# Three gate products of a hybrid decoder layer by seven half-size products, with pooled parts held in DRAM and modulation rows moved

## Chip, cores and metric

The kernel runs on one core of one Trainium2 chip. The metric is device time in microseconds of one execution of the whole layer; the median of three runs of the kernel before is 1093.55 us (1093.42 to 1094.87). Engine names as in the profile: PE is TensorE's matmul, PEld its weight load, DVE VectorE, ACT ScalarE, POOL GpSimd, SP the engine that issues most of the loads.

## The reference, cut to what matters

One layer on 512 tokens of width 1024, all in float32. The two steps around the change are the gated sum of three mixer branches and the modulation vectors:

```python
mod = (silu(c) @ w_ada + b_ada)              # six vectors of 1024
sh1, sc1, g1, sh2, sc2, g2 = split(mod, 6)
h = rms(x, norm1_w) * (1 + sc1) + sh1
z, xbc, dt, q, k, v, u, gates = split(h @ w_in)
...                                          # SSD, dilated attention, multi-scale pooling
y_ssd, y_attn = ssd @ w_ssd_out, attn @ w_attn_out
y_pool = (pooled @ w_pool_mix * pool_scale) @ w_pool_out
g_ssd, g_attn, g_pool = split(sigmoid(gates), 3)
x = x + g1 * ((g_ssd * y_ssd + g_attn * y_attn + g_pool * y_pool) @ w_out)
h = rms(x, norm2_w) * (1 + sc2) + sh2
x = x + g2 * (square(relu(h @ w_ff1)) @ w_ff2)
```

Each of the three gates is a product of h (1024 x 512) with 1024 columns of w_in; the kernel does it in two chunks of 512 columns.

## The kernel before, in words

**Products.** Activations lie feature by token: 8 blocks of 128 x 512 for 1024 features. Every float32 operand is kept as two parts, a rounded high part and the low difference (hh and hl for h), and every product is three matmuls (mm3, line 281): high weight by low input, high by high, low by high. gemm_feat (286) makes 512 output features: it streams the weights in four pairs of 128-row blocks (wstream, 271), and for each of 8 rows k and each of 4 output blocks j it issues three matmuls of 512 columns, 96 in all. A pair of weights is loaded into one of four buffers "raw" (SP's queue, 512 KB), cast by ScalarE to the high part and subtracted by VectorE to the low part, in three buffers each (wh, wl). These steps have a priority 300 instructions ahead of their place (AHEAD), evacuations 200 ahead (SOON).

**The order of work.** The program is written in one order, and a scheduler puts each engine's instructions into a fixed order by priority and readiness. Work that is to lie beside the products stands in a list, side. After each pair of weights wstream calls tick() (252), which takes one entry of side, and as many of a second list, background, as st["pace"] says; flush() (260) takes all that is left in side. Entries of background (ada_later, 239) are the 32 rows of the later modulation vectors (g1, sh2, sc2, g2): a row loads 128 x 1024 of w_ada by SP's queue (512 KB), multiplies by the condition and sums on VectorE, and adds the bias. They begin with the ssd projection, two per tick, and then one per tick (1104, 1106).

**Memory.** Besides fixed tiles there are 49 blocks of 128 x 512 (NBLK). Slots (117) hands out the block that was freed longest ago (`i = self.idle.pop(0)`), in the program's order; a tile's first write waits for the last reader of the tile before it in that block. Four double blocks have the tags L0, L1, N0 and N1, with one buffer each: they hold, one after another, copies of h in the order of residues, the attention output, the weights of the pooling mix (mix_weights, 977: half n in L{n} and N{n}), the modulation rows, and then the weights of the MLP's first product.

**The end of the mixers (1092 to 1110).** After the attention gates GA come the two halves of the pooling input (pool, 954, whose window sums run on VectorE), with the rest of the SSD beside them. pool_mix(gi) (987) makes two blocks of 12 matmuls in all per group of windows, and splits them by ScalarE and VectorE into ph_ and pl_: 16 blocks that stay until the pool projection. Then follow, for each of two chunks, the gate GS, flush(), and project(w_ssd_out), and for each of two chunks the gate GP and project(w_pool_out). gate (730) is gemm_feat and a Sigmoid on the way out; project (734) is gemm_feat, a product with the gate and a sum into the 8 blocks "mixed".

**Seven products.** The MLP does six of its eight chunks of w_ff1 by seven products of half-size blocks in place of eight (seven_products, 1302): with the input sums that input_sums (1283) makes once into 16 blocks tx and ty, and with sums of weight blocks in L and N, 7 x 24 = 168 matmuls of 256 columns make a chunk. A chunk needs all four of its weight tiles (two in L0 and L1, two in raw). The sums of the input are four pieces (rows k and k + 4): six steps and four splits each, and four blocks for the time being.

Of the kernel before, what the change touches and what calls it, by code (L numbers as in the profile page):

```python
# [98 lines left out]
def kernel(ctx: ExitStack, tc: tile.TileContext, a: dict, out: bass.AP, dbg=None):  # L99
# [139 lines left out]
    def ada_later(part, k):  # L239
        def go():  # L240
            o = modv[:, part - 2, k : k + 1]
            w = exp.tile([P, 2, T], F32, tag=("L0", "L1", "N0", "N1")[k % 4], name=uid("wada"))
            nc.sync.dma_start(w, a["w_ada"][part * 8 + k].rearrange("p (i t) -> p i t", i=2))
            V.scalar_tensor_tensor(w, w, 1.0, crow2, ALU.mult, ALU.mult, accum_out=o)
            V.tensor_tensor(o, o, vc("b_ada", part * 8 + k), ALU.add)
        return go


    background = [ada_later(part, k) for part in (2, 3, 4, 5) for k in range(8)]
    side, st, edges = [], {}, []  # L250

    def tick():
        fs = side[:1] + background[: st.get("pace", 0)]
        del side[:1], background[: st.get("pace", 0)]

        with tc.issue_after(edges[0].ins), tc.issue_after(edges[1].ins):
            for f in fs:
                f()
# [468 lines left out]

    mixed, mh, ml = [], [], []

    def gate(c, ch):  # L730
        ps = gemm_feat(w_in, 8, c + ch, hh, hl)
        return evac(ps, "sg", AF.Sigmoid)
# [254 lines left out]
    def pool_mix(gi):  # L987
        wh, wl = mixw[gi]
        for m in range(2):
            ps = psm("mix")  # L990
            cs = slice(m * P, (m + 1) * P)
            for k in range(2):
                mm3(ps, wh[:, k, cs], wl[:, k, cs], dh[2 * gi + k], dl[2 * gi + k], k == 0, k == 1)
            x, y = blk("poolh", F32R), blk("pooll", F32R)
            S.activation(x, ps, AF.Copy, scale=vc("pool_scale", gi * 2 + m))
            V.scalar_tensor_tensor(y, ps, vc("pool_scale", gi * 2 + m), x.bitcast(F32), ALU.mult, ALU.subtract)
            free(ps)
            ph_.append(x)
            pl_.append(y)
# [4 lines left out]
    def pieces(gen):  # L1004

        def step():
            next(gen, None)
        return step

    def do(gen, n):  # L1010
        side.extend([pieces(gen)] * n)
# [48 lines left out]
    for gi in (1, 2):  # L1060
# [7 lines left out]
        scores(gi, qs, rq, ks)  # L1068
    vals.append(take_v(gemm_tok(w_in, 8, VV, hh, hl)))
# [24 lines left out]
    show("oT", [h.bitcast(F32) for h in oh + ol])  # L1094
    for half in range(2):
# [4 lines left out]
        call(pool_mix, 2 * half + 1)  # L1100
    for ch in range(2):
        sg = gate(GS, ch)
        flush()
        st["pace"] = 2
        project(a["w_ssd_out"], 8, ch, yh, yl, sg)
        st["pace"] = 1
    show("yn", [h.bitcast(F32) for h in yh + yl])
    show("pool", [h.bitcast(F32) for h in ph_ + pl_])
    for ch in range(2):
        sg = gate(GP, ch)  # L1110
# [28 lines left out]
    halves = (slice(0, T // 2), slice(T // 2, T))  # L1139
# [13 lines left out]
    with tc.manual_schedule(engines={E.DVE, E.Activation, E.PE}):  # L1153
# [61 lines left out]
        ta, tb = halves  # L1215
# [39 lines left out]
    full, (ta, tb) = slice(0, T), halves  # L1255
# [20 lines left out]

    tq = []

    def input_sums():
        for k in range(4):
            t1, t2, x, y = (blk("tq") for _ in range(4))
            V.tensor_tensor(t1, gh[k].bitcast(F32), gl[k].bitcast(F32), ALU.add)
            V.tensor_tensor(t2, gh[k + 4].bitcast(F32), gl[k + 4].bitcast(F32), ALU.add)
            V.tensor_tensor(x[:, ta], t1[:, tb], t1[:, ta], ALU.subtract)
            V.tensor_tensor(x[:, tb], t2[:, tb], x[:, ta], ALU.subtract)
            V.tensor_tensor(y[:, ta], t2[:, tb], t1[:, tb], ALU.subtract)  # L1290
            V.tensor_tensor(y[:, tb], t2[:, ta], x[:, tb], ALU.subtract)
            tq.append((split(x, "tx"), split(y, "ty")))
            free(t1, t2, x, y)

    def in_b(row, ts):
        return lambda k: (gh[4 * row + k][:, ts], gl[4 * row + k][:, ts])

    def in_t(n):
        ts = halves[n % 2]
        return lambda k: tuple(t[:, ts] for t in tq[k][n // 2])  # L1300

    def seven_products(w, ch):

        L, N, H = [], [], []
        quarters = lambda t: t.rearrange("p i (n c) -> p (i n) c", n=2)
        lo, hi = ta, tb
        with tc.high_priority(offset=AHEAD):
            for m in range(2):
                L.append(exp.tile([P, 2, T], F32, tag=f"L{m}", name=uid("rawl")))
                H.append(raws.tile([P, 2, T], F32, tag="raw", name=uid("raw")))  # L1310
                nc.sync.dma_start(L[m], w[ch, m])
                nc.sync.dma_start(H[m], w[ch, 2 + m])

            def parts(srcs):

                wh = wsp.tile([P, 2, T], F32R, tag="wh", name=uid("wh"))
                wl = wsp.tile([P, 2, T], F32R, tag="wl", name=uid("wl"))
                outs = [(wh, wl)] if len(srcs) == 1 else [(quarters(wh)[:, 2 * m : 2 * m + 2, :], quarters(wl)[:, 2 * m : 2 * m + 2, :]) for m in range(2)]
                for x, (h, l) in zip(srcs, outs):
                    S.copy(h, x)  # L1320
                    V.tensor_tensor(l, x, h.bitcast(F32), ALU.subtract)
                return wh, wl

            a00 = parts([L[m][:, :, lo] for m in range(2)])
            for m in range(2):
                n = exp.tile([P, 2, T], F32, tag=f"N{m}", name=uid("wsum"))
                V.tensor_tensor(n[:, :, lo], L[m][:, :, hi], H[m][:, :, hi], ALU.add)
                V.tensor_tensor(L[m][:, :, hi], L[m][:, :, lo], L[m][:, :, hi], ALU.subtract)
                V.tensor_tensor(n[:, :, hi], n[:, :, lo], L[m][:, :, lo], ALU.subtract)
                V.tensor_tensor(L[m][:, :, lo], H[m][:, :, lo], n[:, :, hi], ALU.subtract)  # L1330
                N.append(n)

        def pair(p, cols):
            return [tuple(t[:, i, cols] for t in p) for i in range(2)]

        def quarter(p):
            return [tuple(quarters(t)[:, i, :] for t in p) for i in range(4)]

        def product(ps, k0, ws, b, first=False):
            for k, (wh, wl) in enumerate(ws, k0):  # L1340
                xh, xl = b(k)
                for j in range(2):
                    o, cs = ps[:, j * 256 : j * 256 + 256], slice(j * P, (j + 1) * P)
                    for n, (x, y) in enumerate(((wh, xl), (wh, xh), (wl, xh))):
                        mm(o, lhsT=x[:, cs], rhs=y, start=first and k == 0 and j == 0 and n == 0, stop=k == 3 and n == 2, skip_group_check=True)  # L1345

        def keep(ps):
            with tc.high_priority(offset=SOON):
                t = blk("keep")
                S.copy(t, ps)  # L1350
            return t

        rs = [blk("relu") for _ in range(4)]

        def add(j0, ts, x, y):
            with tc.high_priority(offset=SOON):
                for j in range(2):
                    c = slice(j * 256, j * 256 + 256)
                    V.tensor_tensor(rs[j0 + j][:, ts], x[:, c], y[:, c], ALU.add)
            free(x, y)  # L1360

        X, Z = acc(), acc()
        product(X, 0, quarter(a00), in_b(0, ta), first=True)
        p1 = keep(X)
        for m in range(2):
            with tc.high_priority(offset=AHEAD):
                s12 = parts([N[m]])
            product(Z, 2 * m, pair(s12, lo), in_t(0), first=True)
            if m == 1:
                p5 = keep(Z)  # L1370
            product(X, 2 * m, pair(s12, hi), in_t(1))
        u2 = keep(X)
        with tc.high_priority(offset=AHEAD):
            a01 = parts([H[m][:, :, lo] for m in range(2)])
        Y = acc()
        product(Y, 0, quarter(a01), in_b(1, ta), first=True)
        add(0, ta, Y, p1)
        for m in range(2):
            with tc.high_priority(offset=AHEAD):
                s43 = parts([L[m]])  # L1380
            product(X, 2 * m, pair(s43, hi), in_t(2))
            if m == 1:
                u3 = keep(X)
            product(Z, 2 * m, pair(s43, lo), in_b(1, tb))
        add(0, tb, Z, u2)
        add(2, tb, u3, p5)
        with tc.high_priority(offset=AHEAD):
            a11 = parts([H[m][:, :, hi] for m in range(2)])
        product(X, 0, quarter(a11), in_t(3))
        with tc.high_priority(offset=SOON):  # L1390
            for j in range(2):
# [92 lines left out]
```

## Time and profile before

| | |
|---|---|
| median of three runs | 1093.55 us (1093.42 to 1094.87) |
| the profiled execution | 1093.37 us |
| its span, first to last instruction | 1091.5 us |
| PE busy | 1086.0 us, 99% of the span |
| DVE busy | 711.5 us, 65% |
| ACT busy | 514.9 us, 47% |
| POOL busy | 12.1 us, 1% |
| moved by DMA | 133.97 MB, mean 123 GB/s |

How to read the answers. A row of the chain, or of a timeline, begins with its start and its length in us. A row of a tile or line gives the engine, the operation, out<-in, the count, then min/median/max of one in ns, and the first and last start in us. A row of waits is "who waited <- for whom: us in total, times, longest". In a table of windows each engine has its busy us and count, in the order PE, PEld, DVE, ACT, POOL; then come the TensorE clock granted (1.00 is full), the share of time in which the DMA engines were busy, and GB/s. A row of DMA issues ends with KB each and the median us from issue to landing. Several engines work at the same time, and busy time of one that nobody waits for costs nothing.

### The profile page before, as it was taken

How to read it: one execution, taken by the hardware profiler on the slowest of the kernel's cores; microseconds unless marked ns; L12 is line 12 of the kernel's file. 1: busy time of each engine (PE TensorE's matmuls, PEld its weight loads, DVE VectorE, ACT ScalarE, POOL GpSimd, SP SyncE). 2: the span in 40 equal slices, each digit the busy share in tenths (PEclk: the TensorE clock that was granted, in tenths of full speed). 3: DMA queues.
4: the chain of work that ended last, by engine and by line, in shares of the span. 5: the costliest groups of instructions: out<-in, count | busy, mean ns of one | idle time of the engine just before them, and what ended most of it. 6: DMA issues, size and time to landing. Idle time of an engine off the chain costs nothing.

```text
span 1091.5 us, 14798 instructions
## 1 busy us (share of the span) xinstructions
PE 1086.0 (99%) x5806; PEld 927.9 (85%) x5806; DVE 711.5 (65%) x1285; ACT 514.9 (47%) x833; POOL 12.1 (1%) x26
## 2 busy tenths in 40 slices
PE   9999999999999999999999999999999999999998
PEld 7878888888887888888888888899889989989987
DVE  8955744461555846678886655567687587587664
ACT  8965875543544943745522123354344334335330
POOL 0000000000100010000000000000000000000000
PEclk9999999999999999999999999999999999999999
DMA  9732223222432243223387655360214224134032
GB/s 352 296 97 91 68 80 112 77 78 78 135 97 78 87 142 100 78 78 102 135 310 251 226 174 169 96 216 2 89 47 155 77 78 141 59 110 136 20 117 77
DMA packets 41034, 133.97 MB, mean 123 GB/s; under 512 B 4851, under 2 KB 5619, under 8 KB 40965
## 3 DMA queue, kind: packets, MB, share of 16 engines
q1 hardware_dynamic: 38480, 126.08, 34.7%
q0 software_dynamic: 1760, 5.77, 1.7%
q10 hardware_dynamic: 724, 1.18, 0.3%
q8 instruction: 45, 0.74, 0.3%
q14 instruction: 25, 0.20, 0.0%
HBM read 130.89 MB, written 2.13 MB: 122 GB/s over the span
## 4 chain that ended last, share of the span: by engine, by line
PE 98%; DVE 1%; issue 0%; ACT 0%; DVEq 0%
PE psacc L282 25%; PE psacc L283 25%; PE psacc L284 25%; PE psacc L1345 11%; PE psacc L522 4%; PE psS L601 1%; PE psy L918 1%; PE pso L717 1%; PE psyo L926 1%; PE pspT L698 1%; PE pso L715 1%; PE psqT L580 0%; PE pskT L585 0%; PE psst L877 0%; PE pswarm L393 0%; PE psmix L283 0%
## 5 line engine op out<-in xcount | busy, mean ns | idle before, releaser
L268 DVE TENSOR_TENSOR wl<-raw,wh 128x1024 fp32r<-128x1024 f32 x140 | 171.0, 1222 | 193.1 <-ACT wh L268 192.8
L268 ACT CAST wh<-raw 128x1024 fp32r<-128x1024 f32 x140 | 146.8, 1049 | 282.0 <-PE psacc L283 183.4
L282 PE MATMUL psacc<-hl,wh 128*128 128x512 f32 x416 | 166.3, 400 | 0.1
L283 PE MATMUL psacc<-hh,wh 128*128 128x512 f32 x416 | 162.0, 389 | 0.0
L284 PE MATMUL psacc<-hh,wl 128*128 128x512 f32 x416 | 162.0, 390 | 0.0
L283 PE MATMUL psacc<-ah,wh 128*128 128x512 f32 (+1 forms) x260 | 100.4, 386 | 0.0
L282 PE MATMUL psacc<-al,wh 128*128 128x512 f32 (+1 forms) x260 | 100.4, 386 | 0.0
L284 PE MATMUL psacc<-ah,wl 128*128 128x512 f32 (+1 forms) x260 | 100.3, 386 | 0.0
L282 PEld LDWEIGHTS psacc<-hl,wh 128*128 128x128 f32 x416 | 78.2, 188 | 17.2 <-issue 1.2
L283 PEld LDWEIGHTS psacc<-hh,wh 128*128 128x128 f32 x416 | 78.2, 188 | 16.9 <-issue 1.4
L284 PEld LDWEIGHTS psacc<-hh,wl 128*128 128x128 f32 x416 | 78.1, 188 | 16.6
L282 PE MATMUL psacc<-wl,rh 128*128 128x512 f32 x192 | 77.2, 402 | 0.0
L283 PE MATMUL psacc<-wh,rh 128*128 128x512 f32 x192 | 75.2, 392 | 0.0
L284 PE MATMUL psacc<-wh,rl 128*128 128x512 f32 x192 | 75.1, 391 | 0.0
L284 PEld LDWEIGHTS psacc<-ah,wl 128*128 128x128 f32 x260 | 48.8, 188 | 9.9
L282 PEld LDWEIGHTS psacc<-al,wh 128*128 128x128 f32 x260 | 48.9, 188 | 9.7
L283 PEld LDWEIGHTS psacc<-ah,wh 128*128 128x128 f32 x260 | 48.9, 188 | 9.7
L1405 DVE SCALAR_TENSOR_TENSOR xr<-psacc,modv,xr 128x512 f32<-128x512 f32 (+1 forms) x65 | 44.7, 740 | 18.5 <-PE psacc L284 18.5
L284 PEld LDWEIGHTS psacc<-wh,rl 128*128 128x128 f32 x192 | 36.1, 188 | 7.6
L282 PEld LDWEIGHTS psacc<-wl,rh 128*128 128x128 f32 x192 | 36.1, 188 | 7.4 <-ACT qT L581 0.2
L283 PEld LDWEIGHTS psacc<-wh,rh 128*128 128x128 f32 x192 | 36.1, 188 | 6.8
L1345 PE MATMUL psacc<-gh,wl 128*128 128x256 f32 x144 | 40.8, 283 | 0.0
(406 smaller groups left out, 2344.1 us busy)
## 6 DMA issues: line engine op xcount, KB each, us to landing
raw<-in_w_in_dram SPq DMA_DIRECT2D x80, 512.0 KB, 3.5
raw<-in_w_ff_dram SPq DMA_DIRECT2D x52, 512.0 KB, 3.9
wada<-in_w_ada_dram SPq DMA_DIRECT2D x46, 512.0 KB, 5.2
rawl<-in_w_ff_dram SPq DMA_DIRECT2D x12, 512.0 KB, 3.4
wst<-in_w_in_dram SPq DMA_DIRECT2D x16, 256.0 KB, 7.8
M<-prow POOLq DMA_DIRECT2D x16, 256.0 KB, 3.9
raw<-in_w_ssd_out_dram SPq DMA_DIRECT2D x8, 512.0 KB, 3.5
raw<-in_w_pool_out_dram SPq DMA_DIRECT2D x8, 512.0 KB, 3.5
```

Source lines behind the costliest of these rows:

```text
L268: edges[:] = S.copy(wh, raw), V.tensor_tensor(wl, raw, wh.bitcast(F32), ALU.subtract)
L282: mm(ps, lhsT=wh, rhs=xl, start=first, stop=False)
L283: mm(ps, lhsT=wh, rhs=xh, start=False, stop=False)
L284: mm(ps, lhsT=wl, rhs=xh, start=False, stop=last)
L522: mm(ps[j], lhsT=t[:, j, :], rhs=w, start=first, stop=last)
L601: mm(so[b], lhsT=qT[:, b * P : (b + 1) * P], rhs=kT[:, (b + 1) * P - n : (b + 1) * P], start=True, stop=True)
L698: nc.tensor.transpose(tp[:, i : i + P], pt[half][:, i : i + P], ident)
L715: mm(od, lhsT=vs[kb][:, hs], rhs=pT[b // 2][:, cs : cs + P], start=(b == 0), stop=False, skip_group_check=True)
L717: mm(ov[:, b, :], lhsT=vs[b][:, hs], rhs=pT[0][:, b * P : (b + 1) * P], start=False, stop=(gi == 2 and b == 3), skip_group_check=True)
L918: mm(yp[half * 64 : half * 64 + 64, cs], lhsT=X[c][:, (2 * j + half) * 64 : (2 * j + half + 1) * 64], rhs=Ms[half][:, cs], start=True, sto ...
L1345: mm(o, lhsT=x[:, cs], rhs=y, start=first and k == 0 and j == 0 and n == 0, stop=k == 3 and n == 2, skip_group_check=True)
L1405: V.scalar_tensor_tensor(xT[d][:, ts], p[:, : ts.stop - ts.start], modv[:, 3, d : d + 1], xT[d][:, ts], ALU.mult, ALU.add)
```

## The change

Four edits. The gates GS, 1 and GP, 0 and GP, 1 are made by seven_products, with sums of hh and hl that are appended to side as four entries (the first joined with pool_mix(3)). seven_products and input_sums are moved up, take their inputs as arguments, and call tick() four times a chunk; the MLP uses the same functions. pool_mix sends each of its 16 blocks to DRAM by POOL's queue and frees it, and again() loads them ahead of the GP gates. The modulation rows are loaded by halves into two blocks each, at most three rows under way, one per tick from the first V product on. The flush behind the gate GS, 0 now stands behind its projection.

```diff
-    def ada_later(part, k):
-        def go():
-            o = modv[:, part - 2, k : k + 1]
-            w = exp.tile([P, 2, T], F32, tag=("L0", "L1", "N0", "N1")[k % 4], name=uid("wada"))
-            nc.sync.dma_start(w, a["w_ada"][part * 8 + k].rearrange("p (i t) -> p i t", i=2))
-            V.scalar_tensor_tensor(w, w, 1.0, crow2, ALU.mult, ALU.mult, accum_out=o)
-            V.tensor_tensor(o, o, vc("b_ada", part * 8 + k), ALU.add)
-        return go
+    rows, loaded = [(part, k) for part in (2, 3, 4, 5) for k in range(8)], []
+    def ada_piece():
+        if len(loaded) == 2 or not rows:
+            part, k, wa = loaded.pop(0)
+            d = small([P, 2], "dot", 4)
+            for i in range(2):
+                V.scalar_tensor_tensor(wa[i], wa[i], 1.0, crow[i], ALU.mult, ALU.mult, accum_out=d[:, i : i + 1])
+            free(*wa)
+            V.scalar_tensor_tensor(modv[:, part - 2, k : k + 1], d[:, 0:1], d[:, 1:2], vc("b_ada", part * 8 + k), ALU.add, ALU.add)
+        if rows:
+            part, k = rows.pop(0)
+            wa = [blk("wa") for _ in range(2)]
+            for i in range(2):
+                nc.sync.dma_start(wa[i], a["w_ada"][part * 8 + k][:, i * T : (i + 1) * T])
+            loaded.append((part, k, wa))
+    background = [ada_piece] * 34
...
+    def input_sums(xh, xl):
+        tq = []
+        def piece(k):
+            def go():
+                t1, t2, x, y = (blk("tq") for _ in range(4))
+                V.tensor_tensor(t1, xh[k].bitcast(F32), xl[k].bitcast(F32), ALU.add)
+                V.tensor_tensor(t2, xh[k + 4].bitcast(F32), xl[k + 4].bitcast(F32), ALU.add)
+                V.tensor_tensor(x[:, ta], t1[:, tb], t1[:, ta], ALU.subtract)
+                V.tensor_tensor(x[:, tb], t2[:, tb], x[:, ta], ALU.subtract)
+                V.tensor_tensor(y[:, ta], t2[:, tb], t1[:, tb], ALU.subtract)
+                V.tensor_tensor(y[:, tb], t2[:, ta], x[:, tb], ALU.subtract)
+                tq.append((split(x, "tx"), split(y, "ty")))
+                free(t1, t2, x, y)
...
+    def gate(c, ch, tq=None, last=False):
+        if tq is None:
+            return evac(gemm_feat(w_in, 8, c + ch, hh, hl), "sg", AF.Sigmoid)
+        rs = seven_products(w_in, c + ch, hh, hl, tq, last)
+        for r in rs:
+            S.activation(r, r, AF.Sigmoid)
+        return rs
...
-            ph_.append(x)
-            pl_.append(y)
+            for t, l in ((x, ph_), (y, pl_)):
+                l.append(dp.tile([P, T], F32, name=uid("pool")))
+                nc.gpsimd.dma_start(l[-1], t.bitcast(F32))
+                free(t)
...
+    st["pace"] = 1
     vals.append(take_v(gemm_tok(w_in, 8, VV, hh, hl)))
...
+    tq, sums = input_sums(hh, hl)
     for half in range(2):
         call(mix_weights, half)
         pool(half)
         rest(2)
         call(pool_mix, 2 * half)
-        call(pool_mix, 2 * half + 1)
-    for ch in range(2):
-        sg = gate(GS, ch)
-        flush()
-        st["pace"] = 2
-        project(a["w_ssd_out"], 8, ch, yh, yl, sg)
-        st["pace"] = 1
+        if half == 0:
+            call(pool_mix, 1)
+    side.append(lambda: (pool_mix(3), sums[0]()))
+    side.extend(sums[1:])
+    sg = gate(GS, 0)
+    project(a["w_ssd_out"], 8, 0, yh, yl, sg)
+    flush()
+    sg = gate(GS, 1, tq)
+    project(a["w_ssd_out"], 8, 1, yh, yl, sg)
+    def again(l, name):
+        for i, d in enumerate(l):
+            l[i] = blk(name, F32R)
+            nc.gpsimd.dma_start(l[i], d)
+    again(ph_, "poolh")
+    again(pl_, "pooll")
     for ch in range(2):
-        sg = gate(GP, ch)
+        sg = gate(GP, ch, tq, ch == 1)
         project(a["w_pool_out"], 8, ch, ph_, pl_, sg, last=True)
```

More of the change, by code (lines that the diff above doesn't have):

```diff
@@ L237 @@
     modv = small([P, 4, 8], "modv")
-    def ada_later(part, k):
-        def go():
-            o = modv[:, part - 2, k : k + 1]
-            w = exp.tile([P, 2, T], F32, tag=("L0", "L1", "N0", "N1")[k % 4], name=uid("wada"))
-            nc.sync.dma_start(w, a["w_ada"][part * 8 + k].rearrange("p (i t) -> p i t", i=2))
-            V.scalar_tensor_tensor(w, w, 1.0, crow2, ALU.mult, ALU.mult, accum_out=o)
-            V.tensor_tensor(o, o, vc("b_ada", part * 8 + k), ALU.add)
-        return go
-    background = [ada_later(part, k) for part in (2, 3, 4, 5) for k in range(8)]
+    rows, loaded = [(part, k) for part in (2, 3, 4, 5) for k in range(8)], []
[14 more added lines that the diff above has]
+    background = [ada_piece] * 34
     side, st, edges = [], {}, []
@@ L254, in tick @@
         del side[:1], background[: st.get("pace", 0)]
+        if not fs:
+            return
         with tc.issue_after(edges[0].ins), tc.issue_after(edges[1].ins):
@@ L725, in attn_out @@
         free(op)
-    mixed, mh, ml = [], [], []
-    def gate(c, ch):
-        ps = gemm_feat(w_in, 8, c + ch, hh, hl)
-        return evac(ps, "sg", AF.Sigmoid)
+    halves = ta, tb = slice(0, T // 2), slice(T // 2, T)
+    def input_sums(xh, xl):
[11 more added lines that the diff above has]
+                free(t1, t2, x, y)
+            return go
+        return tq, [piece(k) for k in range(4)]
@@ L734, in project @@
+    mixed, mh, ml = [], [], []
+    def gate(c, ch, tq=None, last=False):
[4 more added lines that the diff above has]
+            S.activation(r, r, AF.Sigmoid)
+        return rs
     def project(w, nk, ch, yh, yl, sg, first=False, last=False):
@@ L997, in pool_mix, with next_of @@
             free(ps)
-            ph_.append(x)
-            pl_.append(y)
+            for t, l in ((x, ph_), (y, pl_)):
+                l.append(dp.tile([P, T], F32, name=uid("pool")))
+                nc.gpsimd.dma_start(l[-1], t.bitcast(F32))
+                free(t)
         free(*dh[2 * gi : 2 * gi + 2], *dl[2 * gi : 2 * gi + 2])
     yh, yl, dh, dl, ph_, pl_ = [], [], [], [], [], []
-    def pieces(gen):
+    def next_of(gen):
         def step():
@@ L1010, in do @@
     def do(gen, n):
-        side.extend([pieces(gen)] * n)
+        side.extend([next_of(gen)] * n)
     def call(f, *args):
@@ L1099 @@
         call(pool_mix, 2 * half)
-        call(pool_mix, 2 * half + 1)
-    for ch in range(2):
-        sg = gate(GS, ch)
-        flush()
-        st["pace"] = 2
-        project(a["w_ssd_out"], 8, ch, yh, yl, sg)
-        st["pace"] = 1
-    show("yn", [h.bitcast(F32) for h in yh + yl])
-    show("pool", [h.bitcast(F32) for h in ph_ + pl_])
-    for ch in range(2):
-        sg = gate(GP, ch)
+        if half == 0:
[13 more added lines that the diff above has]
+    again(pl_, "pooll")
+    for ch in range(2):
+        sg = gate(GP, ch, tq, ch == 1)
         project(a["w_pool_out"], 8, ch, ph_, pl_, sg, last=True)
@@ L1137, in resident @@
         return res
-    halves = (slice(0, T // 2), slice(T // 2, T))
     ops = gemm_feat(a["w_out"], 8, 0, mh, ml)
@@ L1213, in scale @@
             return r
-        ta, tb = halves
         for j in range(4):
@@ L1252 @@
     show("h2", [h.bitcast(F32) for h in gh + gl])
-    full, (ta, tb) = slice(0, T), halves
+    full = slice(0, T)
     acts = {}
@@ L1274, in square_relu @@
         parts_of(c, rs)
[L1281 to L1391, printed above, removed]
-                S.copy(rs[2 + j][:, ta], X[:, j * 256 : j * 256 + 256])
-        free(X)
-        return rs
@@ L1396, in first_chunk @@
     def first_chunk(c):
-        rs = seven_products(a["w_ff1"], c)
+        rs = seven_products(a["w_ff1"], c, gh, gl, tq, c == 7)
         for r in rs:
@@ L1429 @@
     square_relu(1, [[(p, full)] for p in gemm_feat(a["w_ff1"], 8, 1, gh, gl)])
-    input_sums()
+    tq, pieces = input_sums(gh, gl)
+    for f in pieces:
+        f()
     second(0)
```

91 lines of the change are left out of this document (added).

## The prediction

> **What bounds the kernel now.** I read the page first (engines, the chain that ended last), then the chain piece by piece, the waits of TensorE, and 20 us windows around the gates.
>
> ```profile
> span 1091.5 us, 14798 instructions
> PE 1086.0 (99%) x5806; PEld 927.9 (85%) x5806; DVE 711.5 (65%) x1285; ACT 514.9 (47%) x833; POOL 12.1 (1%) x26
> PEclk9999999999999999999999999999999999999999
> PE 98%; DVE 1%; issue 0%; ACT 0%; DVEq 0%
> ```
> ```profile
> PE pswarm L393 <- DVE ones L362: 1.1, 1, 1.1
> ```
>
> TensorE is the bound: 98% of the chain is its own work, its clock is full in every slice, and its longest wait for another engine in the whole span is 1.1 us, at the start. So time is won only by fewer or shorter matmuls, and any new wait of TensorE is lost in full. The profiled execution took 1093.37 us, its span and 1.9 us around it; the median of the runs is 1093.55. I work from 1093.37.
>
> **The matmuls of a gate.** A gate and its projection have 96 matmuls of 512 columns each. Between the Sigmoid evacuations of two gates lies one of each:
>
> ```profile
> 588.48 1.96 ACT L321 ACTIVATE sg<-psacc 128x512 f32<-128x512 f32 x3 [2.57 <-PE psacc L284]
> ...
> 632.00 1.96 ACT L321 ACTIVATE sg<-psacc 128x512 f32<-128x512 f32 x3 [2.57 <-PE psacc L284]
> ```
> ```profile
> 813.47 20.37 PE psacc L1345 x168
> ...
> 1024.07 20.33 PE psacc L1345 x168
> ```
>
> (632.00 - 588.48) / 2 = 21.76 us a gate, 0.2267 us a matmul. The MLP already does six blocks by seven products: 168 matmuls of 256 columns in 20.33 us, 0.121 each, stalls of some 0.2 us included. Half the columns cost 0.53 of the time, so 7/8 of the columns give 0.934 of it: 1.43 us saved per gate, for three gates **-4.3 us**. This is the whole possible gain, 0.4%.
>
> The Trainium skill (TensorE: Matmul & The Clock Gate, Back-to-back issue gap) gives a warm matmul N/2.4 + 2.5 ns. By it, as an estimate, a gate would fall from 20.7 to 18.4 us and three gates would save 7.1 us; the trace disagrees with its constant (226.7 ns where it has 215.8), and the trace is used.
>
> **What the gate GS, 1 waits for.** The first converted gate needs three things that its twin in the MLP has long before: its second low weight tile, the sums of the inputs, and VectorE's time. I place them on a clock whose zero is the last matmul of pool_mix(3), directly ahead of the gate. That order follows from the side queue: with the entries of the kernel before, GS, 0 takes two rests, pool_mix(0) and pool_mix(1); the ssd projection then takes mix_weights(1), two rests and pool_mix(2); flush() takes pool_mix(3) with the first piece of sums, and the other three pieces. A pool_mix is 12 matmuls, 12 x 0.2267 = 2.72 us, so pool_mix(2) ends at -2.72.
>
> First, the weights. mix_weights(1) sits in the tiles L1 and N1 until pool_mix(3) has read them, and L1 is the gate's second weight tile. The trace shows this very wait for the rows that used these tiles before:
>
> ```profile
> SPq L243 <- PE psmix L284: 8.8, 2, 8.3
> ```
> ```profile
> rawl<-in_w_ff_dram SPq DMA_DIRECT2D x12, 512.0 KB, 3.4
> M<-prow POOLq DMA_DIRECT2D x16, 256.0 KB, 3.9
> out_dram<-xr ACTq DMA_DIRECT2D x4, 256.0 KB, 2.1
> ```
>
> So L1 lands at about +3.5. Its half of the first product (cast 0.6, difference 0.7) is there at about +4.9, where TensorE wants it at +1.44; the sums N1 and their parts follow.
>
> Second, the blocks. The allocator hands out the block freed longest ago. At the flush, 8 blocks hold mixed and 16 the normed SSD, so 25 of 49 are idle; in order of release, 5 are of pool_mix(1), 8 of pool_mix(2) (four of them being spilled), 4 the ssd projection's sg, 8 of pool_mix(3) (four spilled). Eight are taken per piece and four returned. So piece 0 can be computed early but its low parts go to blocks that pool_mix(2) spills; piece 1 begins in the last of these; piece 2 needs blocks that pool_mix(3) spills; piece 3 follows. Pool parts leave TensorE's bank so:
>
> ```profile
> 541.05 1.29 ACT L995 ACTIVATE poolh<-psmix,vec 128x512 fp32r<-128x512 f32 x2
> ```
> ```profile
> 541.80 1.41 DVE L996 SCALAR_TENSOR_TENSOR pooll<-psmix,vec,poolh 128x512 fp32r<-128x512 f32 x2 [0.82 <-ACT poolh L995]
> 566.73 1.37 DVE L738 TENSOR_TENSOR sg<-psacc,sg 128x512 f32<-128x512 f32 x2
> 568.01 0.68 DVE L745 TENSOR_TENSOR sg<-sg,sg 128x512 f32<-128x512 f32 x1
> 568.61 1.28 DVE L738 TENSOR_TENSOR sg<-psacc,sg 128x512 f32<-128x512 f32 x2
> ```
>
> Each takes about 0.7 on ScalarE and then 0.7 on VectorE, and a spill is between the 2.1 us of the 256 KB output and the 3.9 of POOL's loads; no row has a store from POOL, and I take 3.3, nearer to the same queue. pool_mix(2)'s last low part is done at about -1.2 and its block free at +2.1: piece 1 cannot begin before. pool_mix(3)'s last is free at about +5.
>
> Third, VectorE's time, which decides:
>
> ```profile
> L1286 DVE TENSOR_TENSOR tq<-gh,gl x4: 682/688/689, 759.2 to 800.9; 128x512 f32<-128x512 f32 x4
> L1288 DVE TENSOR_TENSOR tq<-tq x4: 417/420/424, 762.0 to 806.5; 128x256 f32<-128x256 f32 x4
> L310 DVE TENSOR_TENSOR txl<-tq,txh x4: 681/691/693, 764.0 to 808.3; 128x512 fp32r<-128x512 f32 x4
> ```
> ```profile
> 770.88 2.50 DVE L1272 TENSOR_TENSOR relu<-relu 128x512 f32<-128x512 f32 x4 [1.28 <-ACT relu L1270]
> ...
> 803.45 1.28 DVE L1321 TENSOR_TENSOR wl<-rawl,wh 128x512 fp32r<-128x512 f32 x2
> ...
> 809.24 1.23 DVE L1321 TENSOR_TENSOR wl<-wsum,wh 128x1024 fp32r<-128x1024 f32 x1 [0.26 <-ACT wh L1320]
> ```
>
> A 512-column step is 0.69 alone and 0.62 in a row (2.50 / 4), a 256-column one 0.42 and about 0.34. A piece has four of the first kind and four of the second: 4 x 0.62 + 4 x 0.34 = 3.8 us. What VectorE must do from about -0.8 on, before the low part of piece 3's tx is there: pieces 1 to 3, 3 x 3.8 = 11.4, less the last low part, 10.8; piece 0's two low parts, 1.2; pool_mix(3)'s two, 1.4; for m = 1 the part of a00 0.6, four steps of sums 2.5 and their part 1.2, together 4.3. In all 17.7, and 1.3 more if the fourth product's weights (a01) are split in between: done at +16.9 to +18.2. The steps that could go ahead of their blocks are in that count because VectorE has no hole left once it has begun.
>
> TensorE, undisturbed, wants that part at 24 + 24 + 6 matmuls x 0.120 = +6.5. The fourth product (24 matmuls, 2.9 us) needs no sums and can be put ahead: +9.4. So TensorE stands for 18.2 - 9.4 = 8.8 us, or 16.9 - 6.5 = 10.4 if it is not put ahead. If low parts of tx are put before those of ty and L1's steps fall in holes, some 4 us of the 17.7 go behind: 5 us. I take **+8.5 us**, between 5 and 11. The later gates find sums and weight tiles ready, like the MLP's blocks: 0.
>
> **The rows.** 32 rows leave the span from 541 us on, where nothing waited for them: 0. They come as 34 ticks from the first V product to the first pair of weights of GA, 0, one per tick:
>
> ```profile
> L244 DVE SCALAR_TENSOR_TENSOR wada<-wada,crow x32: 1216/1220/1226, 544.9 to 664.5; 128x1024 f32<-128x1024 f32 x32
> L244 DVE DVE_READ_ACCUMULATOR wada<-wada,crow x32: 80/83/85, 546.1 to 665.6; 128x1 f32 x32
> L373 DVE SCALAR_TENSOR_TENSOR wada<-wada,crow x2: 685/686/686, 13.6 to 14.2; 128x512 f32<-128x512 f32 x2
> ```
> ```profile
> 340.00:360.00 20.00, 20.00 (x89) 16.00 (x88) 11.88 (x22) 13.28 (x26) 0.00 (x0) 1.00 0.27 80
> 360.00:380.00 20.00, 20.00 (x117) 16.27 (x116) 18.67 (x33) 19.75 (x32) 0.00 (x0) 1.00 0.25 79
> 380.00:400.00 20.00, 20.00 (x117) 16.24 (x116) 11.51 (x18) 8.91 (x12) 2.66 (x5) 1.00 0.45 141
> 540.00:560.00 20.00, 20.00 (x90) 16.56 (x89) 16.50 (x31) 7.21 (x11) 0.00 (x0) 1.00 0.78 273
> 560.00:580.00 20.00, 20.00 (x90) 16.57 (x89) 15.21 (x27) 3.75 (x4) 0.00 (x0) 1.00 0.83 290
> ```
>
> A row by halves is 2 x (0.69 + 0.08) and a small step of 0.15, 1.7 us instead of 1.45. VectorE (the third busy column) has room for three rows, 5.1 us, in 20 us as full as 340 to 360; the fullest, 360 to 380, would need 18.67 + 5.1 = 23.8. The 3.8 over pass into 380 to 400, where 11.51 + 5.1 leave 3.4. The heads' products wait for VectorE's masks there, so between 0 and 3.8 us come onto the path; other weights' matmuls can stand in front, and I take **+0.5**. On SP's queue, 64 loads of 256 KB go past the weights' loads; DMA share is 0.25 to 0.45 there: 0.
>
> **Spill and reload.** POOL is idle here (0.00 in the windows from 540 us). Sixteen reloads:
>
> ```profile
> 286.14 2.12 POOL L898 DMA_DIRECT2D M<-prow  x4 [0.56 <-PE pso L717]
> ```
>
> 0.53 each to issue. Five go to blocks free before the ssd projection, eleven wait for blocks freed at its end: 11 x 0.53 + 3.9 = 10 us, beside gate GP, 0 with 20.3: hidden with 10 us to spare, 0; POOL's queue holds nothing else by then. Were they to land twice as slowly as the M loads, still 0.
>
> **Sum:** 1093.37 - 4.3 + 8.5 + 0.5 = **1098.1 us**; the stall's bounds alone give 1094.6 to 1100.6.
>
> **The rivals.** (1) The sums and weights are ready in time, and the gates run like the MLP's blocks: 1093.37 - 4.3 + 0.5 = 1089.6. For it: VectorE loses 16 rows, 23 us, from 545 to 600, so there is a hole just before the flush. Against: nothing of pieces 1 to 3 but a step or two has a block then. It decides if the hand-over of blocks leaves two pieces more to the time before -5.4, when pool_mix(2) starts. Chance 0.25. (2) A part of this: tx first, much put ahead; a stall of 2 to 4 us, 1091.6 to 1093.6. Chance 0.17. (3) Forecast, stall of 5 to 11: 0.46. (4) The clock. TensorE has no gap over about a microsecond in this trace after the start, and its clock never falls. The new gaps are of 3 us or more; if the clock halves for one product of 24 matmuls, its 2.9 us become 5.8: 1101.0. Chance 0.06. The Trainium skill (TensorE: Matmul & The Clock Gate, What's actually happening) states such a gate, with half rate after an idle window of about 3.4 us; no run here shows it yet. (5) The rows delay the heads by the whole 3.8, on top of the forecast: 1101.4. Chance 0.06.
>
> **How the numbers follow.** Measurement can tell 0.2% here, 2.2 us: faster is under 1091.4, slower over 1095.7. Faster 0.26 (the first rival and a little of the second), same 0.17 (most of the second and the forecast's low edge), slower 0.57 (the rest). The range 1090.0 to 1101.5 leaves out the lower half of the first rival, 0.13, and the worst of the last two, 0.06. The forecast's own range is 1094.6 to 1100.6.
>
> **What would show it.** Right: after the four pool_mix's end, TensorE waits in the first seven-product gate for VectorE (tx low parts, weight differences), in sum 5 to 11 us; L1's load is issued at pool_mix(3)'s last matmul; VectorE is full from there for 15 us or more; the two GP gates take 20.3 us each; no wait on reloads. Wrong: the first seven-product gate takes under 22 us, or TensorE waits elsewhere (psy in 360 to 400, poolh in the pool projection).

## The result, and the profile after

The changed kernel takes 1104.72 us (median of 4, 1104.01 to 1104.87), the kernel before 1094.03 beside it: a ratio of 1.0096, with a 95% interval of 1.0078 to 1.0113. It is slower, as forecast, but by 10.7 us instead of 4.6, and outside the range. The page of its profiled execution, engines, clock and chain:

```profile
span 1102.9 us, 15616 instructions
...
PE 1087.0 (99%) x6022; PEld 937.8 (85%) x6022; DVE 761.6 (69%) x1441; ACT 536.9 (49%) x877; POOL 29.2 (3%) x58
...
PEclk9999999999999999999998999999999999999999
...
PE 79%; issue 16%; DVE 2%; DMA 1%; POOL 1%; ACT 0%; SPq 0%; POOLq 0%; DVEq 0%; ACTq 0%
```

TensorE was 98% of the chain before and is 79% now, but this is not the loss. The chain goes back from the gate's start over a spill to POOL's queue, and counts as "issue" the time in which that queue had nothing to do: 171 us in eight pieces from 386 to 567 us. TensorE was busy meanwhile (147.86 of the 148 us from 398 to 546), and gs1_plain below, which is faster than the kernel before, has such a chain too (83% and 14%). PE's busy share reads 99% because the loss is about 1% of the span: its idle time rose from 5.5 to 15.9 us, and 9.1 us of that lie in the second SSD gate. One slice has a clock below full, the one from 579 to 607 us. The chain of waits shows the gates by seven products as pieces, and ahead of the first the spill that VectorE stood for:

```profile
569.18 4.62 DMA pool<-pooll
...
594.04 10.55 PE psacc L811 x84
...
604.59 0.23 PE psacc L293
...
626.38 20.33 PE psacc L811 x168
...
668.49 20.29 PE psacc L811 x168
```

The two pool gates are one unbroken piece each, of 20.33 and 20.29 us. The second SSD gate has such a piece only for its last half. By the start of its first matmul, 569.87, and that of the projection behind it, 604.4, it takes 34.6 us: 12.8 more than the 21.76 of a gate before and 14.2 more than its twins. (The length of a gate is measured in this way below too.) So the span: +12.8 in this gate, -2.8 in the two others, +0.4 in the first SSD projection, +0.9 ahead of it (0.3 of that ahead of anything changed), 11.3 of the 11.4 us that it grew.

What TensorE waited for between 560 and 610 us, by the view of the waits:

```profile
PEld psacc L811 <- DVE txl L321: 4.9, 2, 3.2
...
PEld psacc L811 <- ACT wh L786: 4.0, 2, 3.2
```

The same stretch in 5 us windows (columns: PE, PEld, DVE, ACT, POOL busy, granted clock, DMA share, GB/s):

```profile
570.00:575.00 5.00, 2.19 (x19) 1.98 (x17) 3.30 (x6) 1.72 (x3) 1.87 (x4) 1.00 0.96 311
575.00:580.00 5.00, 3.58 (x14) 3.00 (x14) 5.00 (x10) 2.39 (x5) 0.00 (x0) 0.55 0.24 98
580.00:585.00 5.00, 4.62 (x22) 4.41 (x21) 5.00 (x11) 1.61 (x3) 0.00 (x0) 0.50 0.01 3
585.00:590.00 5.00, 3.56 (x27) 3.35 (x26) 2.94 (x5) 3.03 (x4) 0.00 (x0) 0.92 0.04 11
590.00:595.00 5.00, 2.00 (x17) 1.79 (x16) 4.64 (x10) 1.24 (x2) 0.59 (x2) 1.00 0.72 235
```

Three things stand in these lines. From 570 to 575 the DMA engines are at 0.96 and VectorE is idle for a third of the time; then VectorE is full; and the clock is at half from 575 to 585. The timeline gives the single steps:

```profile
569.84 0.33 SPq L777 DMA_DIRECT2D rawl<-in_w_in_dram  x1
...
573.83 1.29 DVE L753 TENSOR_TENSOR tq<-hh,hl 128x512 f32<-128x512 f32 x2 [1.69 <-DMA pool<-pooll]
574.48 0.62 ACT L786 CAST wh<-rawl 128x512 fp32r<-128x512 f32 x1 [3.21 <-DMA rawl<-in_w_in_dram]
575.15 0.38 PE L811 MATMUL psacc<-hl,wh 128*128 128x256 f32 x1 [2.97 <-ACT wh L786]
...
576.76 0.41 PE L811 MATMUL psacc<-hl,wh 128*128 128x256 f32 x1
576.97 0.41 PE L811 MATMUL psacc<-hh,wh 128*128 128x256 f32 x1
...
586.39 1.05 ACT L786 CAST wh<-rawl 128x1024 fp32r<-128x1024 f32 x1 [2.09 <-PE psacc L811]
587.47 1.23 DVE L787 TENSOR_TENSOR wl<-rawl,wh 128x1024 fp32r<-128x1024 f32 x1 [1.90 <-ACT wh L786]
...
589.45 1.23 DVE L787 TENSOR_TENSOR wl<-rawl,wh 128x1024 fp32r<-128x1024 f32 x1 [0.16 <-ACT wh L786]
590.59 0.42 DVE L823 TENSOR_TENSOR r<-psacc,keep 128x256 f32<-128x256 f32 x1
...
591.86 0.42 DVE L823 TENSOR_TENSOR r<-psacc,keep 128x256 f32<-128x256 f32 x1
...
593.30 0.69 DVE L321 TENSOR_TENSOR txl<-tq,txh 128x512 fp32r<-128x512 f32 x1
```

The load of L1 is issued at 569.84, the end of pool_mix(3), as forecast, and lands 4.6 us later. VectorE's first sum waits for a spill. At 576.97 matmuls start 0.21 us apart, not 0.12: half rate. From 585.6 to 587.5 VectorE stands in a ring of the three engines: its queue has a weight difference ahead of piece 2's low part; that waits for ScalarE's cast; the cast waits for a buffer that TensorE, at half rate until 585.8, reads only then; and TensorE itself stands from 587.9 to 589.35 for that low part. The last low part is ready at 594.0. The transfers of the stretch 560 to 575, with the microseconds from issue to landing in the last column:

```profile
pool<-poolh POOLq DMA_DIRECT2D x4, 256.0 KB, 4.0
pool<-pooll POOLq DMA_DIRECT2D x4, 256.0 KB, 4.9
rawl<-in_w_in_dram SPq DMA_DIRECT2D x1, 512.0 KB, 4.6
```

### The profile page after: what moved, and what is told of

Same layout as the page of the kernel before. It is cut to its first block, busy times and chain, and to the rows that moved or that the text cites. A ratio compares the mean times of both kernels' runs of the same rounds, so it can differ in the third digit from the quotient of the medians.

```text
span 1102.9 us, 15616 instructions
## 1 busy us (share of the span) xinstructions
PE 1087.0 (99%) x6022; PEld 937.8 (85%) x6022; DVE 761.6 (69%) x1441; ACT 536.9 (49%) x877; POOL 29.2 (3%) x58
## 4 chain that ended last, share of the span: by engine, by line
PE 79%; issue 16%; DVE 2%; DMA 1%; POOL 1%; ACT 0%; SPq 0%; POOLq 0%; DVEq 0%; ACTq 0%
PE psacc L293 18%; PE psacc L295 18%; PE psacc L294 18%; PE psacc L811 16%; PE psacc L533 4%; PE psS L612 1%; PE pso L728 1%; PE pso L726 1%; POOL pool L1146 1%; PE psqT L591 0%; PE pskT L596 0%; PE pspT L709 0%; DMA xT<-in_x_dram 0%; DMA pool<-pooll 0%; POOL M L1044 0%
## 5 line engine op out<-in xcount | busy, mean ns | idle before, releaser
L293 PE MATMUL psacc<-hl,wh 128*128 128x512 f32 x320 | 128.8, 403 | 0.2 <-ACT pT L710 0.2
L294 PE MATMUL psacc<-hh,wh 128*128 128x512 f32 x320 | 124.6, 390 | 0.0
L295 PE MATMUL psacc<-hh,wl 128*128 128x512 f32 x320 | 124.5, 390 | 0.0
L293 PEld LDWEIGHTS psacc<-hl,wh 128*128 128x128 f32 x320 | 60.1, 188 | 13.4 <-issue 1.2
L294 PEld LDWEIGHTS psacc<-hh,wh 128*128 128x128 f32 x320 | 60.2, 188 | 13.3 <-issue 1.4
L295 PEld LDWEIGHTS psacc<-hh,wl 128*128 128x128 f32 x320 | 60.1, 188 | 12.9
L787 DVE TENSOR_TENSOR wl<-rawl,wh 128x512 fp32r<-128x512 f32 (+1 forms) x36 | 33.7, 954 | 35.6 <-ACT wh L786 35.6
L786 ACT CAST wh<-rawl 128x512 fp32r<-128x512 f32 (+1 forms) x36 | 29.2, 833 | 51.3 <-PE psacc L294 28.7
L786 ACT CAST wh<-wsum 128x1024 fp32r<-128x1024 f32 x18 | 19.0, 1053 | 72.0 <-PE psacc L294 69.5
L811 PE MATMUL psacc<-txl,wh 128*128 128x256 f32 x144 | 42.0, 292 | 4.4 <-DVE txl L321 4.4
```

Source lines behind the costliest of these rows:

```text
L293: mm(ps, lhsT=wh, rhs=xl, start=first, stop=False)
L294: mm(ps, lhsT=wh, rhs=xh, start=False, stop=False)
L295: mm(ps, lhsT=wl, rhs=xh, start=False, stop=last)
```

## The experiments

Theory at the outset: all of the loss is lateness at the start of the second SSD gate (tile L1, blocks under spills, VectorE's chain), with the clock's fall on top. Rivals: the spill's traffic or the seven products cost time wherever they stand; the rows cost it; one of the three causes is all of it.

**gs1_plain** and **rows_only**: one part undone, one part alone.

```diff
-    sg = gate(GS, 1, tq)
+    sg = gate(GS, 1)
```

> The second SSD gate is computed as in the kernel before (96 matmuls of 512 columns); everything else, the sums of the inputs ahead of it too, is as in the changed kernel. Theory (the loss is TensorE's wait at the start of the first gate by seven products, because its weight tile, its blocks and VectorE are late): the gate goes from 34.6 us to about 21.8, so 1104.7 - 12.8 = 1091.9 us, between 1091 and 1093 if the sums delay a weight split or two; clock 1.00 in all windows. Rival (traffic of the spill or seven products among other work cost the time, wherever they stand): over 1097 us, with waits in the SSD projection or the pool gates.

Measured: 1091.77 us, ratio 0.9986 (0.9977 to 0.9995); the gate takes 21.76 us, the clock is 1.00. The sums are still computed and the spills still made beside it, so neither costs anything that the time shows. The loss belongs to this gate's start alone, and two gates by seven products are a gain.

rows_only is the kernel before with the new ada_piece, its 34 ticks and the pace of 1 from the first V product.

> The kernel before with nothing changed but the modulation rows: by halves in two blocks, one piece per pair of weights from the first V product on. Theory: they cost what the changed kernel shows ahead of its second SSD gate, 0.9 to 1.3 us: 1094.9 to 1095.3 us. Rival 1: they cost nothing and the 0.9 comes from the other parts: 1094.0. Rival 2: taking 23 us of VectorE's work out of 541 to 665 us speeds something up there: under 1093.4.

Measured: 1093.95 us, ratio 1.0003 (0.9995 to 1.0012): no difference that can be told. In its trace a given matmul starts 0.17 us later than before at 100 us, where nothing is changed yet, and 0.66 at 240 and 0.73 at 480: half a microsecond, nearly all between 190 and 240 us. In the changed kernel the same points read 0.33, 0.82 and 0.88.

**hold**, **spill_act**, **fill**: one cause at a time taken out of the changed kernel. First the tiles of the mix weights:

```diff
-        ... exp.tile([P, 2, T], F32R, tag=f"{x}{n}", ...) for x in "LN")
+        ... exp.tile([P, 2, T], F32R, tag="LN"[n] + x, ...) for x in "01")
```

> The changed kernel, with the first mix weights in the tiles L0 and L1 and the second in N0 and N1, so that the low weights of the second SSD gate can be loaded while pool_mix(2) and pool_mix(3) still run; N0 and N1 are free at pool_mix(3)'s end. Theory (VectorE's chain of sums decides, the tile held is only the first of the waits): the first gap of 3.2 us goes, most of the later gaps stay: 1099 to 1103 us. Rival 1 (the tile held is the cause of it all, the clock's fall included): 1091 to 1093. Rival 2 (it is hidden behind the sums altogether): 1104 to 1105.

Measured: 1107.10 us, ratio 1.0119 (1.0104 to 1.0135), the gate 38.1 us. Slower, which neither theory had. The waits of TensorE in that gate:

```profile
PEld psacc L811 <- DVE txl L321: 5.5, 2, 3.4
PEld psacc L811 <- ACT wh L786: 3.4, 1, 3.4
PEld psacc L811 <- DVE wl L787: 1.5, 1, 1.5
```

L0 and L1 are there, but N0 and N1 are now held to the end of pool_mix(3), and the compiled order of VectorE has the sums of both weight tiles and four splits, from 569.8 to 578.1, ahead of all that remains of the inputs' sums. The wait changed its name from a tile to the queue behind it. The held tile alone is not the cause.

```diff
-                nc.gpsimd.dma_start(l[-1], t.bitcast(F32))
+                nc.scalar.dma_start(l[-1], t.bitcast(F32))
```

> The changed kernel, with the stores of the pooled parts issued from ScalarE's queue instead of POOL's. Theory (VectorE stood idle for 1.7 us at 572.2 until a spill that took 4.6 us had landed, and the blocks come free sooner by a queue whose 256 KB store took 2.1 us): 1.5 to 2.5 us less, 1102 to 1103. Rival (blocks are not on the path): 1104.7; or slower by 1 to 2 us, where ScalarE's casts stand behind a store that waits for VectorE.

Measured: 1102.48 us, ratio 1.0082 (1.0069 to 1.0096); the gate 32.3 us, 2.2 less. The same eight stores land so:

```profile
pool<-poolh ACTq DMA_DIRECT2D x4, 256.0 KB, 2.3
pool<-pooll ACTq DMA_DIRECT2D x4, 256.0 KB, 2.9
```

That is 2 us sooner than from POOL. The gain is what the theory gives, though the intervals of the two kernels overlap here.

```diff
-        product(X, 0, quarter(a00), in_b(0, ta), first=True)
+        product(X, 0, quarter(a00)[:2], in_b(0, ta), first=True)
+        if ch == GS + 1:
+            W = acc()
+            for i in range(14):
+                mm(W, lhsT=xh[0][:, lo][:, :P], rhs=xh[1], start=i == 0, stop=i == 14 - 1)
+            free(W)
+        product(X, 2, quarter(a00)[2:], in_b(0, ta))
```

> The changed kernel, with 14 more matmuls of 512 columns (3.2 us) into an idle PSUM bank between the halves of the first product of the second SSD gate, where TensorE had its gap of 3.2 us; their result is used by nothing. Theory (the gap makes the clock fall, and some 34 matmuls at 0.213 instead of 0.120 us cost about 3 us): the clock stays at 1.00 in that gate, and the time falls to 1101.5 to 1103 in spite of the added work. Rival 1 (VectorE's chain sets the end, a slow TensorE is hidden in waits that would be there anyway): clock 1.00 and 1104.2 to 1105. Rival 2 (low density, not the gap, lowers the clock): clock still 0.5 between 575 and 585 us, 1104.7 or more.

Measured: 1103.72 us, ratio 1.0096 (1.0081 to 1.0112), that of the changed kernel to the digit; the gate 32.9 us in the trace. Its windows:

```profile
570.00:575.00 5.00, 4.38 (x24) 3.46 (x23) 2.83 (x5) 1.33 (x3) 1.62 (x3) 1.00 0.98 289
575.00:580.00 5.00, 4.06 (x20) 3.68 (x20) 5.00 (x9) 2.47 (x5) 0.00 (x0) 0.72 0.24 99
580.00:585.00 5.00, 4.31 (x34) 3.89 (x33) 5.00 (x12) 2.14 (x4) 0.00 (x0) 0.94 0.01 3
```

The filled gap takes most of the clock's fall away (0.72 and 0.94 for 0.55 and 0.50). The median lies between the two expectations, and by the ratios nothing is gained. The trace says otherwise: 10 steps at half rate are left of 30 (0.093 us more each, so 1.9 us less), VectorE's queue has the same order as in the changed kernel, its 1.9 us in the ring are gone, and the gate is 1.7 us shorter. So half rate was not all hidden: a slow TensorE gave the weight buffer back late and held up VectorE. Single executions point the same way. Those of spill_act took 1101.7 us twice, at a mean clock of 0.998, and 1103.2 and 1103.6 at 0.995.

**early**, **beside**, **sums_late**, **late_act**: the side entries at other places. early leaves out the rests and brings the second mix weights forward:

```diff
-    for half in range(2):
-        call(mix_weights, half)
-        pool(half)
-        rest(2)
-        call(pool_mix, 2 * half)
-        if half == 0:
-            call(pool_mix, 1)
+    call(mix_weights, 0)
+    pool(0)
+    call(pool_mix, 0)
+    call(mix_weights, 1)
+    pool(1)
+    call(pool_mix, 1)
+    call(pool_mix, 2)
     side.append(lambda: (pool_mix(3), sums[0]()))
     side.extend(sums[1:])
```

> All three gates by seven products, but the side entries are called without rests, in the order pool_mix(0), the second mix weights, pool_mix(1), pool_mix(2), then pool_mix(3) with the first piece of sums and the other three pieces: one per pair of weights of the first SSD gate and the first SSD projection, nothing left for the flush. Theory (lateness of the weight tile, of blocks and of VectorE makes the stall, and the gaps lower the clock): the second SSD gate takes 20.3 to 21 us, clock 1.00, time 1104.7 - 14.2 = 1090.5 us, up to 1092.5 if VectorE is too full in the first SSD projection. Rival (the first gate by seven products waits for something else, such as the memory traffic of the spills or its own weights): the gate stays over 27 us and the time over 1097.

Measured: 1097.93 us, ratio 1.0039 (1.0026 to 1.0051). The gate is at 22.0 us, but the first SSD projection at 27.0 (21.76 in the kernel before). Its third PSUM bank had just been pool_mix(2)'s. From the timeline and the windows of early:

```profile
546.08 0.39 PE L295 MATMUL psacc<-ynh,wl 128*128 128x512 f32 x1
549.83 0.69 PE L293 MATMUL psacc<-ynl,wh 128*128 128x512 f32 x1 [3.36 <-DVE pooll L1142]
550.31 0.63 PE L294 MATMUL psacc<-ynh,wh 128*128 128x512 f32 x1
```
```profile
550.00:555.00 5.00, 5.00 (x16) 3.93 (x17) 3.60 (x7) 1.24 (x2) 1.08 (x2) 0.66 0.53 203
```

TensorE waits for VectorE to empty that bank; VectorE had stood 3.6 us at a weight sum whose load had not landed, then 1.5 us at a spill. After the gap eight matmuls come 0.43 us apart instead of 0.23. So lateness is the cause in the gate, and a new wait took part of the gain back; the time is the rival's (over 1097), its reason is not.

beside keeps pool_mix(2) away from the change of banks: one rest after pool_mix(1), then pool_mix(2), pool_mix(3) with piece 0, piece 1, pieces 2 and 3 in one tick.

> All three gates by seven products; the side entries are put so that no pool_mix ends right ahead of a change of PSUM banks: pool_mix(0), the second mix weights, pool_mix(1) and one rest in the first SSD gate; pool_mix(2), pool_mix(3) with the first piece of sums, the second piece, and the third and fourth together in the first SSD projection; nothing left for the flush. Theory (the whole loss is lateness at the start of the second SSD gate): that gate takes 20.3 to 21.5 us at a clock of 1.00 and the first SSD projection 21.8 to 22.5, time 1104.7 - 14.2 + 0 to 1.5 = 1090.5 to 1092. Rival (VectorE has no room for the sums in the first SSD projection, so that the stall only moves there): over 1094.

Measured: 1094.71 us, ratio 1.0011 (1.0002 to 1.0020). The time is the rival's (over 1094), but the stall has not moved to the projection: that takes 21.8 us, the gate 24.3, with gaps of 3.2 us for a low part of the sums and 0.8 for ScalarE's copy out of a PSUM bank. sums_late has the pool mixes as beside and all four pieces in the flush; late_act is the same with the spills on ScalarE's queue.

> As the run before in its pool_mix entries (all done by the middle of the first SSD projection, so that weight tiles and blocks are free and the spills over long before the second SSD gate), but the four pieces of sums come in the flush, directly ahead of that gate. It measures VectorE's throughput alone. Theory (VectorE's 15 us of sums and weight sums decide): the gate takes 25 to 29 us, time 1095 to 1099. Rival (the tile and the blocks held by the pool mix were the cause): under 22 us, 1090.5 to 1092. Where the scheduler moves pieces ahead by itself, the gate lies between.

> All pool_mix by the middle of the first SSD projection, the four pieces of sums in the flush, spills from ScalarE's queue. If the 8.0 us that TensorE waited with POOL's spills are VectorE's throughput alone, this is the same within 1 us (1097 to 1098.5); if spills were still in it, 2 us or more less.

Measured: sums_late 1097.88 us, ratio 1.0039 (1.0027 to 1.0052), the gate 28.4; late_act 1096.42, ratio 1.0026 (1.0016 to 1.0035), the gate 25.6. The chain of late_act in the gate is VectorE's from end to end:

```profile
572.24 1.88 DVE sg L891 x3
574.12 1.21 DVE wl L787 x2
...
579.87 1.14 DVE wl L787
...
583.36 0.70 DVE txl L321
584.07 0.04 issue
584.11 10.55 PE psacc L811 x84
```

With tile and blocks out of the way and no half rate, VectorE's throughput alone makes TensorE wait 25.6 - 20.3 = 5.3 us. That is the least of it: this execution took 1094.68 us at a clock of 1.000, the nine others 1095.97 to 1097.07 at 0.998. Of the 2.7 more in sums_late 1.1 are twelve matmuls at half rate; the rest is not told apart from a different order of VectorE's queue. The median of late_act is 1.5 us lower, between its two expectations, so how much the spills were still in sums_late stays open.

**hold_act**: both remedies at once in the changed kernel.

> The changed kernel (two pool_mix at the flush) with both remedies at once: the gate's low weights free early (first mix weights in L0 and L1, second in N0 and N1) and spills from ScalarE's queue. If tile and spill together make the 6 us that the changed kernel loses beyond VectorE's throughput, the gate takes 28 to 29 us and the time is near 1097.9; if VectorE's order of work decides (weight sums of N0 and N1 ahead of the sums of the inputs, as with the tiles alone), it stays at 1102 to 1105.

Measured: 1104.73 us, ratio 1.0102 (1.0087 to 1.0118), the gate 36.2. Tile and spill together give nothing while pool_mix(2) and pool_mix(3) stand directly ahead: the weight sums go ahead of the inputs' sums again.

**ahead**, **ahead_act**, **ahead_hold**, **plain_act**: the search for a version that keeps the gain. ahead puts pieces 0 and 1 ahead of the last spills (shown against early):

```diff
     call(pool_mix, 1)
-    call(pool_mix, 2)
-    side.append(lambda: (pool_mix(3), sums[0]()))
-    side.extend(sums[1:])
+    side.append(sums[0])
+    side.append(lambda: (sums[1](), pool_mix(2)))
+    side.append(lambda: (pool_mix(3), sums[2]()))
+    side.append(sums[3])
```

> All three gates by seven products; the sums come still earlier, so that the first two pieces take blocks that no spill holds: pool_mix(0), the second mix weights, pool_mix(1) and piece 0 of the sums in the first SSD gate; piece 1 with pool_mix(2), then pool_mix(3) with piece 2, then piece 3 in the first SSD projection. Theory (the second SSD gate waits only for pieces of sums that are late): it takes 20.3 to 22 us, the time is 1090.3 to 1092.5, under the kernel before and about 1 us under the kernel with only the two pool gates by seven products. Rival (VectorE is too full around the first SSD projection for 15 us of sums whatever their order): 1093.5 or more, with the stall in the projection or still in the gate.

> The run before with the spills from ScalarE's queue. If the spills still hold blocks that a piece waits for, 1 us less than that run; if not, the same within 0.5 us, or more where ScalarE's casts of weights stand behind a store.

> The run before the last (sums early, spills from POOL) with the first mix weights in the tiles L0 and L1 and the second in N0 and N1. If the tile L1 is no longer on the path, its release some 15 us ahead of the gate being early enough, the same time within 0.5 us; if it is, 1 us or more less.

Measured: ahead 1096.65 us, ratio 1.0030 (1.0018 to 1.0041), the gate 26.7; ahead_hold 1096.60, 1.0033 (1.0021 to 1.0044), 26.3: the tile is off the path. ahead's time is in its rival's range, but a full VectorE was not the reason, as the next run shows. ahead_act 1091.08, ratio 0.9979 (0.9971 to 0.9988), the gate 20.9: 5.6 us from the store's queue, five times what was expected. What VectorE waited for in ahead between 535 and 590 us, and how its stores landed:

```profile
DVE tq L753 <- DMA pool<-pooll: 5.8, 2, 4.2
```
```profile
pool<-poolh POOLq DMA_DIRECT2D x8, 256.0 KB, 4.6
pool<-pooll POOLq DMA_DIRECT2D x8, 256.0 KB, 4.4
```

And the same wait and the stores in ahead_act, and the gate's last piece in ahead and in ahead_act:

```profile
DVE tq L753 <- DMA pool<-pooll: 0.5, 1, 0.5
```
```profile
pool<-poolh ACTq DMA_DIRECT2D x8, 256.0 KB, 2.5
pool<-pooll ACTq DMA_DIRECT2D x8, 256.0 KB, 2.8
```
```profile
578.58 17.98 PE psacc L811 x129
```
```profile
574.69 15.38 PE psacc L811 x126
```

Stores that land 2 us sooner take 5.3 us of this waiting from VectorE. The last unbroken piece then starts 5.7 us behind the gate's first matmul instead of 8.9, and runs at full rate; in ahead the clock fell after TensorE's gaps there, and 25 steps of that piece took 2.5 us more than at 0.12 each. So the 5.8 us between the two gates (26.7 and 20.9) are some 3 of waiting and 2.5 of clock. Does the queue help by itself?

> Only the two pool gates by seven products (the second SSD gate as before), spills from ScalarE's queue. A control for the store's queue where no sum is on TensorE's path. Theory (the queue matters only through blocks that sums wait for): within 0.7 us of the same kernel with spills from POOL, 1091.1 to 1091.8 us. Rival (ScalarE's queue speeds up something by itself): 1 us or more below it, so that the three-gate kernel's lead would not come from its third gate.

Measured: 1091.11 us, ratio 0.9978 (0.9969 to 0.9987). As the theory has it, though just at the edge: 0.7 below gs1_plain, whose interval overlaps it. And it ties with ahead_act: the third gate's 0.9 us (21.76 - 20.9) don't show in the medians. Both beat both kernels of this case; the simpler one needs no sums ahead of the SSD gate.

## Why the prediction was wrong

**What bounds, matmuls of a gate, reload.** Right. The pool gates take 20.33 and 20.29 us where 20.33 was forecast, and no matmul of the pool projections waits for a reload. (In the estimate that is set aside there the shorter gate comes to 18.3 us, not 18.4; nothing hangs on it.)

**Rows.** The size was right (+0.5; half a microsecond, and nothing measurable in the time), the place was not: it lies between 190 and 240 us, and nothing is lost from 360 to 400.

**The stall.** This step failed, by its size: 14.2 us where 8.5 was taken and 11 was the top. The order (L1 issued at pool_mix(3)'s end, blocks under spills, VectorE last) held. Wrong was the sentence that "VectorE has no hole left once it has begun". From 569.87 to 594.0 VectorE worked 20.4 us, where the forecast had 19 less the 0.8 done before, 18.2, and stood 3.8: 1.7 for a spill, which took 4.6 us and not 3.3, and 1.9 in the ring. The work that was left out is the weight differences of the last products (two of 1.23 us) and two sums of results (0.42 each) that the queue has ahead of piece 3. So the last low part came at +24.1 instead of +18.2, and 24.1 - 9.4 (the point to which TensorE can run) = 14.7 is about the stall. VectorE's throughput alone, which the forecast took to decide, is 5.3 us in late_act, with the work in another order and at full clock: the forecast's low edge. How the other 8.9 divide between the tile, the spills and the half rate is left open: taken away one by one in the changed kernel they move the gate by +3.5, -2.2 and -1.7 us in the traces, and in the first two VectorE's queue takes another order, so these don't add.

**"Spill and reload: 0".** The reload, yes. The spill was priced as a transfer beside other work while it was also what holds the blocks. Its queue is worth 5.6 us where the rest is in order (ahead to ahead_act), the clock's share included.

**The rivals.** The clock was given 0.06 as a case of its own. It followed from the forecast's own gaps of 3 us and belonged inside the sum. Its price was put at 2.9; the trace of fill has 1.7, by way of the ring, while the medians show nothing, so its size stays open between nothing and some 2 us. The rival "ready in time" would have been 1089.6; ahead_act, which makes them ready, is at 1091.08.

## What to carry to other kernels

A stall behind an engine whose instructions have a fixed order is not that engine's work: list everything in its queue ahead of the one instruction that is waited for, and for each the semaphore it can itself stand at, since the holes add to the work and may depend on the waiting engine. A block that is given back by a store is free when the store has landed, so the store's queue is a price on the path even when its bandwidth is hidden. And a change that gains 1.4 us a gate is worth making only for the gates whose inputs are ready: two gates gave the whole measurable gain, and the third lost 3 to 15 us wherever its inputs were late (beside to hold, against gs1_plain).

## What the runs showed of the hardware

A 256 KB store from SBUF landed in 4.0 to 4.9 us from POOL's queue and in 2.3 to 2.9 from ScalarE's (medians of after and ahead, of spill_act and ahead_act), in kernels that differ in nothing else. The Trainium skill (DMA: Bandwidth & Descriptors, SWDGE vs HWDGE vs iDMA) says that software on GpSimd computes the descriptors of the one and hardware those of the other, and advises the second for plain transfers; the runs agree (with the stores on ScalarE's queue, in spill_act, 4.20 MB move from the queue that the profile calls software_dynamic to one that it calls hardware_dynamic, and land sooner), and the difference of 2 us is larger than the 0.4 us that the same page's Specifications leave between the two to the first byte.

The clock fell to half beside TensorE's gaps, but not by the length of a single gap. A gap of 3.75 us from start to start was followed by half rate at once (early), so were two of 2.0 and 2.5 us with one matmul between them (ahead) and one of 3.29 a few matmuls behind one of 1.33 (ahead_hold), while single ones of 3.28 and 3.37 us were followed by full rate (the changed kernel at 594.0, late_act at 584.1). The Trainium skill (TensorE: Matmul & The Clock Gate, What's actually happening) has a window of 3.4 us that runs freely and isn't started by the gap, and these runs fit it: inside the span, half clock lasted 3.41 us (early), 6.83 (ahead) or 10.24 (the changed kernel, 575.52 to 585.76), multiples of one length. On the grid that these ends give, the stretch of 3.41 us just ahead of a fall had TensorE busy for 0.14 us (early), 0.45 (the changed kernel), 1.12 (sums_late) and 1.30 (ahead), so it need not be empty; stretches with 1.69 and 1.96 (the changed kernel, 589.17 to 596.0) kept the full clock. Busy time alone does not draw the line, though: in fill the clock fell behind a stretch with 1.84. Full clock came back behind stretches with 3.0 us or more (fill, sums_late, early), and not behind 1.72 (ahead) or 2.54 and 2.64 (the changed kernel).
